# Max pooling over groups of 16: each row load split into two DMAs, issued from SyncE and ScalarE

## The chip, the cores and the metric

The kernel runs on one core of one Trainium2 chip. The metric is the device time of one execution in microseconds (us), given as the median of several runs. The profile is one further execution, recorded by the hardware profiler.

## The reference

The input `x` is 32 x 256 x 4096 in float32 (134.22 MB), and the output is 32 x 256 x 256 (8.39 MB). Each output is the maximum of 16 neighbouring inputs, because 4096 / 256 = 16:

```python
for i in range(output_size):            # 256
    start = int(i * length / output_size)
    end = int((i + 1) * length / output_size)
    result[:, :, i] = np.max(x[:, :, start:end], axis=-1)
```

## The kernel before

All the 2,097,152 windows of W = 16 elements are laid out as 128 partitions x 16,384 windows. The work is cut into 16 chunks of CHUNK = 1024 windows per partition: nine chunks form the first group, six and a last one form the second. Within a group, each partition reads one contiguous piece of memory. A full chunk is one load of 128 rows of 64 KB, 8192 KB in all.

One tile, `sb`, holds everything: a ring with two slots of CHUNK + GAP windows, and behind the ring the pooled results, which stay on the chip until the end. The order of the program is:

- A small first load (line 70) brings the final FIRST = 128 windows of each partition, 1024 KB in rows of 8 KB, into a part of the ring that the first full load does not touch, and `pooled` reduces it. What the last chunk still has to load is then 896 windows per partition, 7168 KB in rows of 56 KB. That is the "last load".
- The loop over `rows` issues 15 full loads and the last load (line 88). Load k goes to slot k % 2. Within the slot it alternates between offset 0 and offset GAP = 152 every second use (`moved`), so that load k + 2 overlaps all but 152 windows of load k, and never touches those 152.
- Each full chunk is reduced by VectorE in two instructions (line 57, inside `pooled`): first the 872 windows that load k + 2 will overwrite, then the 152 that it will not. Load k + 2 can therefore be issued as soon as the larger reduction of load k is done, while the smaller one still runs. Two loads can be outstanding at a time.
- The last load is reduced in one instruction of 896 windows.
- The output leaves in three stores: two large ones from SyncE (line 103: 4608 KB for the first group, 3072 KB for six chunks of the second) behind all loads, and one of 512 KB from ScalarE (line 100) when the last reduction is done.

All loads and the two large stores are issued by SyncE, in the order of the program. ScalarE issues only the last store and computes nothing. The tile framework puts in the waits: a load waits for the reductions that read, and the loads that wrote, what it overwrites, and a reduction waits for the loads that wrote what it reads.

Of the kernel before, what the change touches and what calls it, by code (L numbers as in the profile page):

```python
# [1 line left out]

# [4 lines left out]


@with_exitstack
def kernel(  # L10
    ctx: ExitStack,
    tc: tile.TileContext,
    x: bass.AP,
    output_size: bass.AP,
    out: bass.AP,
):
    nc = tc.nc
    P = nc.NUM_PARTITIONS
    fp32 = mybir.dt.float32

    B, C, L = x.shape
    O = int(output_size)
    assert L % O == 0, (L, O)
    W = L // O
    total = B * C * O // P
    assert B * C * O % P == 0

    xw = x.flatten_outer_dims().rearrange("r (o w) -> (r o) w", w=W)
    ow = out.flatten_outer_dims().rearrange("r o -> (r o)")
    taken = 0  # L30

    def group(n):

        nonlocal taken
        span = slice(taken * P, (taken + n) * P)
        taken += n
        return (
            xw[span].rearrange("(p n) w -> p (n w)", p=P),
            ow[span].rearrange("(p n) -> p n", p=P),
        )  # L40

    CHUNK = 1024
    GAP = 152
    FIRST = 128
    RING = 2 * (CHUNK + GAP) * W


    GROUPS = (9, 6)
    last = CHUNK - FIRST
    assert (sum(GROUPS) + 1) * CHUNK == total and last * (W + 1) <= CHUNK * W  # L50


    pool = ctx.enter_context(tc.tile_pool(name="pool", bufs=1))
    sb = pool.tile([P, RING + total - last], fp32, tag="sb", name="sb")

    def pooled(dst, at, n):
        nc.vector.reduce_max(  # L57
            out=sb[:, dst : dst + n],
            in_=sb[:, at * W : (at + n) * W].rearrange("p (n w) -> p n w", w=W),
            axis=mybir.AxisListType.X,  # L60
        )

    groups = [
        group((loads + (g == len(GROUPS) - 1)) * CHUNK) for g, loads in enumerate(GROUPS)
    ]
    assert taken == total
    x_end, o_end = groups[-1]
    cut = GROUPS[-1] * CHUNK

    nc.sync.dma_start(  # L70
        out=sb[:, CHUNK * W : (CHUNK + FIRST) * W], in_=x_end[:, (cut + last) * W :]
    )
    pooled(RING, CHUNK, FIRST)

    rows, stores = [], []
    at = RING + FIRST
    for (xg, og), loads in zip(groups, GROUPS):
        rows += [(xg, k * CHUNK, CHUNK, at + k * CHUNK) for k in range(loads)]
        if loads:
            stores.append((og[:, : loads * CHUNK], sb[:, at : at + loads * CHUNK]))  # L80
        at += loads * CHUNK
    rows.append((x_end, cut, last, None))

    for k, (xg, a, n, dst) in enumerate(rows):

        moved = k // 2 % 2
        at = k % 2 * (CHUNK + GAP) + moved * GAP
        nc.sync.dma_start(
            out=sb[:, at * W : (at + n) * W], in_=xg[:, a * W : (a + n) * W]
        )  # L90
        if dst is not None:
            mid = CHUNK - GAP if moved else GAP
            parts = [(0, mid), (mid, n)]
            for u, v in parts if moved else parts[::-1]:
                pooled(dst + u, at + u, v - u)
        else:
            assert (at + CHUNK) * W == RING
            pooled(RING - n, at, n)

    nc.scalar.dma_start(out=o_end[:, cut:], in_=sb[:, RING - last : RING + FIRST])  # L100
    tc.no_sync_barrier()
    for dst, src in stores:
        nc.sync.dma_start(out=dst, in_=src)


# [1 line left out]
_INS = ['x', 'output_size']  # L107
_OUTS = [((32, 256, 256), 'float32')]

_NUMBERS = {'output_size': 256}  # L110


# [26 lines left out]
```

## Time and profile before

| quantity | value |
|---|---|
| time, median of 3 runs | 334.65 us (334.64 to 334.85) |
| profiled execution, its own time | 334.95 us |
| span of that execution (first to last instruction) | 333.2 us |
| VectorE (DVE) busy | 276.5 us, 83% of the span |
| DMA queue q1 (SyncE's), share of 16 engines | 98.8% |
| DMA queue q10 (ScalarE's), share of 16 engines | 0.4% |
| bytes read / written | 134.22 MB / 8.39 MB |

The profiled execution spent 1.75 us outside its span, and took 0.30 us more than the median. In the profile, a "packet" is the record of one row moved by one DMA engine, or of the small completion record of 4 bytes that each of the 16 engines writes at the end of a DMA. A full load thus leaves 128 + 16 = 144 packets, eight rows and one completion record per engine. "SPq" and "ACTq" are the instruction streams of SyncE and ScalarE.

### The profile page before, as it was taken

How to read it: one execution, taken by the hardware profiler on the slowest of the kernel's cores; microseconds unless marked ns; L12 is line 12 of the kernel's file. 1: busy time of each engine (PE TensorE's matmuls, PEld its weight loads, DVE VectorE, ACT ScalarE, POOL GpSimd, SP SyncE). 2: the span in 40 equal slices, each digit the busy share in tenths (PEclk: the TensorE clock that was granted, in tenths of full speed). 3: DMA queues.
4: the chain of work that ended last, by engine and by line, in shares of the span. 5: the costliest groups of instructions: out<-in, count | busy, mean ns of one | idle time of the engine just before them, and what ended most of it. 6: DMA issues, size and time to landing. Idle time of an engine off the chain costs nothing.

```text
span 333.2 us, 113 instructions
## 1 busy us (share of the span) xinstructions
DVE 276.5 (83%) x32; POOL 0.2 (0%) x4
## 2 busy tenths in 40 slices
DVE  2009979797997979799797979979797997979994
POOL 0000000000000000000000000000000000000000
DMA  9898989899898989899898989999898989999997
GB/s 378 378 504 378 504 378 496 386 409 472 378 504 378 504 378 496 386 409 472 378 504 378 504 378 488 393 409 472 378 504 378 504 378 488 393 456 434 396 406 323
DMA packets 2880, 142.61 MB, mean 428 GB/s; under 512 B 320, under 2 KB 320, under 8 KB 448
## 3 DMA queue, kind: packets, MB, share of 16 engines
q1 hardware_dynamic: 2736, 142.08, 98.8%
q10 hardware_dynamic: 144, 0.52, 0.4%
HBM read 134.22 MB, written 8.39 MB: 428 GB/s over the span
## 4 chain that ended last, share of the span: by engine, by line
DMA 58%; DVE 36%; DVEq 5%; issue 0%; SPq 0%
DMA sb<-in_x_dram 58%; DVE sb L57 36%; DVEq L134 5%; SPq L70 0%
## 5 line engine op out<-in xcount | busy, mean ns | idle before, releaser
L57 DVE TENSOR_REDUCE sb<-sb 128x872 f32<-128x13952 f32 (+3 forms) x32 | 276.5, 8681 | 51.8 <-DMA sb<-in_x_dram 51.8
L120 POOL MEMSET const-bfloat16-1.0<- 128x1 bf16 x1 | 0.1, 102 | 0.0
L120 POOL MEMSET const-uint8-127<- 128x1 uint8 x1 | 0.1, 101 | 0.0
L120 POOL MEMSET const-float32-0.0<- 128x1 f32 x1 | 0.1, 99 | 0.2 <-issue 0.2
L120 POOL MEMSET const-float32-1.0<- 128x1 f32 x1 | 0.1, 98 | 0.0
## 6 DMA issues: line engine op xcount, KB each, us to landing
sb<-in_x_dram SPq DMA_DIRECT2D x1, 7168.0 KB, 21.6
out_dram<-sb SPq DMA_DIRECT2D x1, 4608.0 KB, 32.1
out_dram<-sb SPq DMA_DIRECT2D x1, 3072.0 KB, 17.7
sb<-in_x_dram SPq DMA_DIRECT2D x1, 1024.0 KB, 5.0
out_dram<-sb ACTq DMA_DIRECT2D x1, 512.0 KB, 4.0
sb<-in_x_dram SPq DMA_DIRECT2D x15, 24.0
```

Of the source, the lines that this page charges most:

```text
L57: nc.vector.reduce_max(out=sb[:, dst : dst + n], in_=sb[:, at * W : (at + n) * W].rearrange("p (n w) -> p n w", w=W), axis=mybir.AxisListT ...
L120: nc = _bacc.Bacc("TRN2", target_bir_lowering=False, num_devices=1)
L134: with _tile.TileContext(nc) as tc:
```

## The change

Every load of the loop goes out as two DMAs: SyncE issues the first half of the windows of each partition, ScalarE the second half. The rows of each DMA are half as long (32 KB, and 28 KB for the last load). The small first load, the reductions and the stores are as before.

```diff
         moved = k // 2 % 2
         at = k % 2 * (CHUNK + GAP) + moved * GAP
-        nc.sync.dma_start(
-            out=sb[:, at * W : (at + n) * W], in_=xg[:, a * W : (a + n) * W]
-        )
+
+        half = n // 2
+        for queue, u, v in ((nc.sync, 0, half), (nc.scalar, half, n)):
+            queue.dma_start(
+                out=sb[:, (at + u) * W : (at + v) * W], in_=xg[:, (a + u) * W : (a + v) * W]
+            )
         if dst is not None:
```

## The prediction

> **What bounds the kernel now.** I read the page first: how busy the DMA engines are, and whether anything else is near its limit.
>
> ```profile
> DVE 276.5 (83%) x32; POOL 0.2 (0%) x4
> ...
> q1 hardware_dynamic: 2736, 142.08, 98.8%
> q10 hardware_dynamic: 144, 0.52, 0.4%
> ```
>
> The 16 DMA engines are busy for almost the whole span, VectorE for 83% of it. The page's chain names 58% DMA and 36% DVE, but that is one ring slot at a time; the chain in order of time shows the period:
>
> ```profile
> 39.83 23.97 DMA sb<-in_x_dram
> 63.80 0.02 issue
> 63.82 14.70 DVE sb L57
> 78.52 0.02 issue
> 78.54 23.96 DMA sb<-in_x_dram
> ```
>
> One slot takes 38.7 us per load. With two slots, a load lands every 19.35 us. Next the windows, to see if the engines rest inside that period (columns: window, DVE busy, POOL busy, PE clock, DMA share, GB/s):
>
> ```profile
> 20.50:39.83 19.33, 14.72 (x2) 0.00 (x0) 1.00 1.00 434
> 39.83:59.18 19.35, 17.27 (x3) 0.00 (x0) 1.00 1.00 434
> ```
>
> They don't: share 1.00, 434 GB/s. Of the 23.97 us from issue to landing, 19.35 are the transfer, and the other 4.6 are mostly queueing behind the load before. That queue is the reserve. A new load's data starts moving about 1.02 us after its issue (the first issue, at 0.72, has its first packet record at 1.75), and the engines write their last row of the load before up to 1.0 us ahead of its landing (records: 43.44 on the first engine to finish, landing 44.45). So a load at 39.83 is ready at 40.85, and the engines run dry at 43.44: **a load may be issued 2.6 us later than now before an engine idles.** VectorE's own reserve is the 2.07 us it waits before each load:
>
> ```profile
> 44.47 17.28 DVE L57 TENSOR_REDUCE sb<-sb 128x872 f32<-128x13952 f32 x2 [2.08 <-DMA sb<-in_x_dram]
> 63.82 17.28 DVE L57 TENSOR_REDUCE sb<-sb 128x872 f32<-128x13952 f32 x2 [2.07 <-DMA sb<-in_x_dram]
> ```
>
> At the start there is no pooling to wait for: SyncE issues the small load and two full loads at once.
>
> ```profile
> 0.72 0.37 SPq L70 DMA_DIRECT2D sb<-in_x_dram  x1
> 1.15 0.90 SPq L88 DMA_DIRECT2D sb<-in_x_dram  x2
> 5.76 2.29 DVE L57 TENSOR_REDUCE sb<-sb 128x128 f32<-128x2048 f32 x1 [5.76 <-DMA sb<-in_x_dram]
> 25.11 14.69 DVE L57 TENSOR_REDUCE sb<-sb 128x872 f32<-128x13952 f32 x1 [17.07 <-DMA sb<-in_x_dram]
> ```
>
> In one queue, load 0 is moved completely before load 1 begins. This order is what the change gives up.
>
> **The change part by part.** *Issues.* ScalarE gains 16 DMA issues, SyncE keeps its 17 loads. An issue of a load took 0.33 to 0.43 us, and only SyncE's own issues follow it, so taking the second half to ScalarE removes nothing from the path: 0 us. ScalarE has no other work; its last store stands behind the last half load, which is issued 37 us earlier. Cover: the 2.6 us above.
>
> *Waits.* Each half load waits for the same large reduction as the whole load did. Each large reduction waits for two semaphores instead of one; the nearest row is a wait instruction of 0.02 to 0.03 us on SyncE, inside VectorE's 2.07 us of idle time: 0 us. If that cover were gone, 16 x 0.03 = 0.5 us.
>
> *Rows.* In the packet records, a 64 KB row follows the one before on its engine after 2.414 us, an 8 KB row after 0.306 us. Two points give 4.8 ns per row and 1.205 us per 32 KB. Per load an engine gets 16 rows instead of 8, and two completion records instead of one: 8 x 4.8 ns + 6 ns = 0.044 us. The engines are the bound, so 16 loads cost 16 x 0.044 = **0.7 us**. Bounds: 0, if two queues hide the step between rows, and 1.4 us, if changing queue costs as much again. I take 0.7.
>
> *The order at the start.* ScalarE leaves the opening barrier 5 ns after SyncE (0.647 against 0.642 in the instruction records), so its half of load 0 goes out together with the small load. Now each engine has two queues with work. No two queues overlap for long in this trace: q10 has only the last store, whose packets start at 330.02, when q1's last one ends. So how they share is unknown, and I bound it. If the engine takes all of a DMA before it changes, the order stays as it was: 0 us. If it takes one row from each queue in turn, the small load's eight rows of 8 KB alternate with eight of 32 KB, and all of load 0's ScalarE half is through when the small load is. ScalarE's queue is then one half load ahead. Load 0's SyncE half next alternates with *load 1's* ScalarE half:
> - small load now through at 4.80 us on the first engine; with eight 32 KB rows (8 x 1.21 = 9.67), at 14.5;
> - then 8 rounds of two 32 KB rows, 19.35 us: load 0 is through at 33.8, or 32.6 if SyncE's row goes first in each round. Before: 24.12. So it lands 8.5 to 9.7 us later, and I take 8.5, as SyncE issues first;
> - VectorE starts on it at 25.11 + 8.5 = 33.6 and is through with 872 windows at 48.3; load 2 goes out then and is ready at 49.35;
> - load 1 ends at 43.5, where it always did, since the bytes are the same. The engines idle **5.8 us** (7.0 at the other end).
>
> After that, load 2's halves start together with equal rows and stay level. VectorE ends load 1 at 50.9 + 14.7 = 65.6, load 3 is ready at 66.6, load 2 lasts until 49.35 + 19.35 = 68.7: cover 2.1 us, so no further idling. Later VectorE waits 2 us per load again, and the tail is shifted as a whole: the last reduction starts at 313.23, when VectorE is through with the chunk before, and the last load has landed 0.3 us earlier (312.95); both move by the same amount.
>
> The sum against the profiled execution: 334.95 + 0.7 + 5.8 = 341.45; less the 0.30 by which it lies over the median, **341.2 us**.
>
> The Trainium skill, "DMA: Bandwidth & Descriptors", section "Issuing engines are not separate DMA queues", speaks against the change: DMAs of several engines run on the same 16 DMA engines and interleave, and only sequencer time is saved. By that rule the gain is nil, and the trace agrees, with 98.8% busy from one queue.
>
> **The rivals.**
>
> *Whole DMAs in turn (not slower).* The engine keeps to one DMA's share (eight rows and the completion record) before it changes queue. Then the order is small load, half, half, as before, and only the rows cost: 334.65 + 0.7 = 335.35 if the step of 4.8 ns stays, 334.65 if it is hidden, 334.75 if it stays but the slow start is filled (the small load's eight rows take 3.05 us from the first packet, against 8 x 0.306 = 2.45, so at most 0.6 is to be had there). It decides from the point where a run of one queue's rows is longer than the 2.6 us of cover. For: on the last engine a q1 row still begins at 329.72, when q10's store, issued at 328.34, could have been there (329.36). Against: this is 0.36 us, less than the time of one row.
> By the Trainium skill, same page, section "Queues, rings and completion order", an engine goes round its queues packet by packet, draining typically 9 to 17 descriptors before it switches. If the nine records of a load's share on an engine are such a packet, this rival holds, with 335.35; if each row is a packet, the forecast does. No run so far shows which.
>
> *Equal bytes.* The queues share by bytes. Then the small load (64 KB per engine) puts ScalarE's queue two 32 KB rows ahead, load 0 lands 2.4 us late, which the cover of 2.6 just takes; a lead of one row may live on to the end. There the last load would land 1.2 us late, the last reduction would end at 329.5, and its store, now waiting until 330.02 for the engines, would be ready at 330.6 or later while nothing else is left to move. Price 0.7 + up to 1.4: 336.8.
>
> *Faster.* Two queues keep each engine fuller. What is to be had: the 0.6 us at the start, and 0.03 us in each of some 12 loads, which take 19.35 in the packet records instead of the first four's 19.32. At most 1.0, less what the rows cost: 334.0. Against it: the share is 1.00 already.
>
> That the change doesn't do what it says can be left out: ScalarE's instruction stream has the 16 loads.
>
> **How the numbers follow.** The measurement can tell about 0.2%, here 0.67 us: under 333.98 is faster, over 335.32 slower. Row by row: 0.50, all slower. Whole DMAs: 0.26, of which 0.13 within 0.2% (rows hidden or the start filled), 0.12 slower by a hair and 0.01 faster. Equal bytes: 0.14, slower. Fuller engines: 0.06, faster. 0.04 for something slower that I don't see, such as a lead of one queue that returns with every load. Faster 0.07, same 0.13, slower 0.80. The forecast's own range is 340.5 (start filled) to 342.6 (7.0 of idling). For 8 in 10 the range must reach down through the two cheaper ways of sharing: 334.7 to 342.4.
>
> **What would show it.** In the profile after: the small load's time to landing goes from 5.0 us to 13 or 14; the first large reduction starts at 33 to 35 instead of 25.11; the DMA row has a gap of about 6 us near 44 to 50 us, and nothing like it later; landings then come every 19.39 us; VectorE waits about 2 us before each load. If the first large reduction starts near 25, the queues don't alternate by rows, and I am wrong by 6 us. If it starts near 27.5, they share by bytes. If load 2 comes late but the gap returns with every pair of loads, the queues do not start level again, and the time is well over 343.

## The result, and the profile after

The changed kernel takes **343.97 us** (343.87 to 344.23, 4 runs), against 334.74 us for the kernel before in the same comparison: 9.23 us more, ratio 1.0275 (95% interval 1.0263 to 1.0288). The forecast was 341.2 us, with a range that ended at 342.4. The sign and the mechanism were right, the size was not. The profiled execution took 343.87 us, with a span of 341.8 us.

The page after, sections 1 and 3 (columns of the queues: packets, MB, share of 16 engines):

```profile
DVE 276.4 (81%) x32; POOL 0.2 (0%) x4
...
q1 hardware_dynamic: 2736, 75.50, 51.6%
q10 hardware_dynamic: 2448, 67.11, 45.6%
```

Together the queues now fill 97.2% of the span instead of 99.2%, and VectorE's work is the same 276 us. Most of the loss is idle DMA time. The page's row of DMA load in 40 slices shows where:

```profile
DMA  7999929999999999999999999999999999999997
```

There is one hole, in the sixth slice. The timeline of the start shows what leads up to it:

```profile
0.73 66.29 ACTq L91 DMA_DIRECT2D sb<-in_x_dram  x4
0.73 0.38 SPq L70 DMA_DIRECT2D sb<-in_x_dram  x1
...
15.24 2.29 DVE L57 TENSOR_REDUCE sb<-sb 128x128 f32<-128x2048 f32 x1 [15.24 <-DMA sb<-in_x_dram]
34.75 34.46 DVE L57 TENSOR_REDUCE sb<-sb 128x872 f32<-128x13952 f32 x4 [17.23 <-DMA sb<-in_x_dram]
71.58 14.69 DVE L57 TENSOR_REDUCE sb<-sb 128x872 f32<-128x13952 f32 x1 [2.36 <-DMA sb<-in_x_dram]
```

The small load's reduction starts at 15.24 us instead of 5.76, and load 0's at 34.75 instead of 25.11. Loads 0 and 1 are then reduced without a pause (34.46 us, four instructions): load 1 was there already. In the chain in order of time, load 2 goes out only when the first large reduction ends:

```profile
49.45 0.02 issue
49.47 22.09 DMA sb<-in_x_dram
71.56 0.02 issue
71.58 14.70 DVE sb L57
86.28 0.02 issue
86.30 24.12 DMA sb<-in_x_dram
```

Load 2 lands after 22.09 us because nothing was queued in front of it. From load 4 on a load takes 24.12 us, so the queue is full again. The windows (columns: window, DVE busy, POOL busy, PE clock, DMA share, GB/s) show the engines before and in the hole:

```profile
33.80:43.60 9.80, 8.85 (x1) 0.00 (x0) 1.00 0.99 428
43.60:50.50 6.90, 6.90 (x2) 0.00 (x0) 1.00 0.13 33
```

From the packet records, no engine has work between 43.93 and 50.42 us. On average an engine rests 6.9 us, and its first 32 KB row afterwards takes 1.66 to 2.13 us instead of 1.21. The span grew by 8.6 us, from 333.2 to 341.8, so 6.9 of it is this rest.

The records of one engine at the hand-over from the small load show how two queues are served (start in us, us, queue, bytes):

```
12.983 0.309 q1  8192    the small load's eighth row
13.289 1.213 q10 32768   the eighth row of ScalarE's half of load 0
14.499 0.009 q1  4       the small load's completion record
14.505 0.009 q10 4       the half load's completion record
14.510 1.213 q1  32768   first row of SyncE's half of load 0
15.720 1.213 q10 32768   first row of ScalarE's half of load 1
```

The queues take turns row by row, an 8 KB row against a 32 KB row. A completion record is a turn of its own: the small load's data is through at 13.29, but its record waits for the other queue's row and is written at 14.50.

### The profile page after: what moved, and what is told of

It is laid out like the page before. It is cut to its first block, busy times and chain, and to the rows that moved or that the text cites. A ratio compares the mean times of both kernels' runs of the same rounds, so it can differ in the third digit from the quotient of the medians.

```text
span 341.8 us, 157 instructions
## 1 busy us (share of the span) xinstructions
DVE 276.4 (81%) x32; POOL 0.2 (0%) x4
## 4 chain that ended last, share of the span: by engine, by line
DMA 59%; DVE 35%; DVEq 4%; issue 0%; SPq 0%
DMA sb<-in_x_dram 59%; DVE sb L57 35%; DVEq L137 4%; SPq L70 0%; DVEq L57 0%
## 6 DMA issues: line engine op xcount, KB each, us to landing
sb<-in_x_dram ACTq DMA_DIRECT2D x15, 4096.0 KB, 24.1
sb<-in_x_dram SPq DMA_DIRECT2D x1, 1024.0 KB, 14.5
```

## The experiments

**Start level.** The small load is split too, so that neither queue gets ahead.

```diff
-    nc.sync.dma_start(
-        out=sb[:, CHUNK * W : (CHUNK + FIRST) * W], in_=x_end[:, (cut + last) * W :]
-    )
+    for queue, u, v in ((nc.sync, 0, FIRST // 2), (nc.scalar, FIRST // 2, FIRST)):
+        queue.dma_start(
+            out=sb[:, (CHUNK + u) * W : (CHUNK + v) * W],
+            in_=x_end[:, (cut + last + u) * W : (cut + last + v) * W],
+        )
```

> The changed kernel, but the small first load is split in two halves like the others (SyncE and ScalarE, eight rows of 4 KB per engine each), so that both queues start level. Theory (the queues take one row in turn, and the small load on SyncE's queue alone lets ScalarE's queue run one half load ahead, which idles the engines once, near 44 to 50 us): load 0 lands near 25 again, no gap, only the dearer rows are left: 335.4 to 336.1 us. Rival (two queues fall out of step by themselves, or cost in every load): the time stays above 340 us.

Measured: 336.41 us against 334.73, ratio 1.0048 (1.0035 to 1.0060). Its timeline:

```profile
25.14 17.28 DVE L57 TENSOR_REDUCE sb<-sb 128x872 f32<-128x13952 f32 x2 [17.31 <-DMA sb<-in_x_dram]
44.59 17.28 DVE L57 TENSOR_REDUCE sb<-sb 128x872 f32<-128x13952 f32 x2 [2.17 <-DMA sb<-in_x_dram]
```

Load 0 is back at 25.14, load 1 at 44.59, and there is no hole. All 16 loads still go out as halves from two engines, so 7.6 of the 9.2 us hang on the order at the start. The rest, 1.68 us, is 0.3 us over the upper end of what was expected.

**Whole loads first.** Loads 0 and 1 whole from SyncE, halves from load 2 on.

```diff
-        for queue, u, v in ((nc.sync, 0, half), (nc.scalar, half, n)):
+        halves = ((nc.sync, 0, half), (nc.scalar, half, n))
+        for queue, u, v in halves if k >= 2 else ((nc.sync, 0, n),):
```

> The changed kernel, but loads 0 and 1 go out whole from SyncE; the halves on two queues begin with load 2. Theory (all of the big loss is the order at the start): first large reduction at 25.1 us, no gap, 335.3 to 336.0 us. Rival (the halves cost in every load): with 14 of 16 loads still in halves, most of the 9.2 us stays, above 341 us.

Measured: 336.26 us against 334.73, ratio 1.0049 (1.0035 to 1.0063). The first large reduction starts at 24.69:

```profile
24.69 17.28 DVE L57 TENSOR_REDUCE sb<-sb 128x872 f32<-128x13952 f32 x2 [17.05 <-DMA sb<-in_x_dram]
```

The total is 0.3 us over the upper end of the expected. 14 loads in halves cost only 1.5 us, so the 9.2 us are not a price paid in every load.

**Halves first.** The opposite: only loads 0 and 1 as halves.

```diff
+        halves = ((nc.sync, 0, half), (nc.scalar, half, n))
+        for queue, u, v in halves if k < 2 else ((nc.sync, 0, n),):
```

> The kernel before, but loads 0 and 1 alone go out as halves from SyncE and ScalarE. Theory: the whole gap is back with only two of 16 loads changed: load 0 lands near 34.8, engines idle 6.6 us and take 0.9 us to come back to speed, 334.7 + 7.5 + 0.1 = 342.3 us. Rival (cost spread over all loads): 2/16 of 9.2 us, 335.9 us.

Measured: 342.63 us against 334.73, ratio 1.0235 (1.0221 to 1.0249): 7.90 us.

```profile
34.78 34.47 DVE L57 TENSOR_REDUCE sb<-sb 128x872 f32<-128x13952 f32 x4 [17.22 <-DMA sb<-in_x_dram]
71.43 14.69 DVE L57 TENSOR_REDUCE sb<-sb 128x872 f32<-128x13952 f32 x1 [2.19 <-DMA sb<-in_x_dram]
```

The changed kernel's start is here to within 0.2 us, with two loads of 16 changed.

**One queue.** Both halves from SyncE, one behind the other.

```diff
-        for queue, u, v in ((nc.sync, 0, half), (nc.scalar, half, n)):
+        for queue, u, v in ((nc.sync, 0, half), (nc.sync, half, n)):
```

> The changed kernel, but both halves of every load go out from SyncE, one behind the other: the same rows and DMAs in one queue, so that nothing is taken in turn. Theory: no gap; the price of 32 KB rows alone, 16 x 0.044 = 0.7 us, 335.4 us; if the further 0.04 us per load that the changed kernel's period shows (19.43 instead of 19.39 us) belongs to the rows and not to changing queue, 335.9 us. Rival (halving the loads is what costs, whatever the queue): above 341 us.

Measured: 335.83 us against 334.73, ratio 1.0029 (1.0018 to 1.0041): 1.10 us for twice the rows and DMAs alone. Two pieces of its chain, two loads apart:

```profile
59.54 23.74 DMA sb<-in_x_dram
...
98.39 23.75 DMA sb<-in_x_dram
```

98.39 - 59.54 = 38.85 us for two loads, 19.43 each, the same as in the changed kernel. The price above the 0.7 us of the forecast belongs to the short rows, not to changing queues. The packet records agree: with one queue a half load takes 9.68 us at first and 9.71 from about 55 us on, and in the changed kernel more than half of the 32 KB rows follow each other after 1.213 to 1.219 us instead of 1.209 from about 90 us on.

The kernel before slows too. On its first engine the completion records of the loads come 19.32 us apart up to 82 us, and 19.35 afterwards. Spread over the eight rows of a load that is about 4 ns per row, and the halves have sixteen: 19.36 us at first, 19.42 to 19.43 later. So the halves cost 0.043 us per load at first, which is what the forecast had, and 0.077 later. From the small load's completion record to that of the last load, the engine that is ahead takes 307.1 us in the kernel before and 308.3 with one queue, 1.2 us more where 0.7 was forecast. Why rows become slower in the course of a run is not known.

**The dose.** If rows are served in turn, load 0 is late by eight of ScalarE's rows, so the loss must follow their length. SyncE takes three quarters, or one quarter, of each load:

```diff
-        half = n // 2
+        half = n * 3 // 4        # the other kernel: n // 4
```

> The changed kernel, split at three quarters: SyncE's rows are 48 KB, ScalarE's 16 KB. Theory (one row in turn, whatever its length): until the small load's eight rows are through, ScalarE's queue moves eight rows of 16 KB, so load 0 is late by half of what it was, 8 x 0.61 = 4.8 us, lands near 29.9, and the engines idle 2.2 us and restart slowly (0.9): 334.7 + 1.1 for the rows + 3.1 + up to 0.4 = 338.9 to 339.3 us. Rival (what counts is that two queues start unequal, or bytes are shared equally): the start does not get cheaper by the shorter rows, 343 to 344 us by the first, 336 to 337 by the second.

> The other way: SyncE's rows are 16 KB, ScalarE's 48 KB. Theory: load 0 is late by 8 x 1.8 = 14.5 us, the engines idle 11.8 us and restart in 0.9: 334.7 + 1.1 + 12.7 + up to 0.4 = 348.5 to 348.9 us. Rivals as for three quarters: 343 to 344, or 336 to 337 us.

Measured, against 334.81: 347.27 us (344.69 to 349.72), ratio 1.0345 (1.0288 to 1.0402), for three quarters; 361.81 us, ratio 1.0789 (1.0768 to 1.0810), for one quarter. Both miss, the first even in the order: a smaller imbalance was slower than the even split. The timeline of the three quarters says why:

```profile
66.96 17.28 DVE L57 TENSOR_REDUCE sb<-sb 128x152 f32<-128x2432 f32 x2 [2.54 <-DMA sb<-in_x_dram]
86.36 17.28 DVE L57 TENSOR_REDUCE sb<-sb 128x152 f32<-128x2432 f32 x2 [2.13 <-DMA sb<-in_x_dram]
108.71 17.28 DVE L57 TENSOR_REDUCE sb<-sb 128x872 f32<-128x13952 f32 x2 [5.07 <-DMA sb<-in_x_dram]
```

Two of the merged lines begin with the 152 windows instead of the 872. In the even split the small reduction also needs only one of the two DMAs, and the large one both, but there the large one comes first in all 15 full loads. With unequal parts the framework's scheduler put the small one first in 7 of the 15. The load that waits for the large reduction then goes out 2.6 us later, which is the whole of the 2.6 us of cover. Load 4's reduction at 108.71 has waited 5.07 us. The four runs lie in two pairs, near 344.8 and 349.7 us, and the trace is of the slower pair; what sets them apart is not shown. In the one-quarter kernel it is worse, since VectorE takes the small reduction of load 1 before the large one of load 0:

```profile
39.63 2.69 DVE L57 TENSOR_REDUCE sb<-sb 128x152 f32<-128x2432 f32 x1 [17.14 <-DMA sb<-in_x_dram]
44.52 31.87 DVE L57 TENSOR_REDUCE sb<-sb 128x152 f32<-128x2432 f32 x3 [2.20 <-DMA sb<-in_x_dram]
```

So both were run again with the order of the reductions held:

```diff
             for u, v in parts if moved else parts[::-1]:
                 pooled(dst + u, at + u, v - u)
+                tc.no_sync_barrier()
```

> The split at three quarters again, with the order of VectorE's reductions held to that of the changed kernel (the larger one first in every load; in the run without this it came second in half of the loads, so that the load after it went out 2.6 us later). Theory (a row in turn, and the swapped order took the cover): load 0 lands near 29.9, one gap of 2.2 us plus 0.9, then none: 338.9 to 339.3 us. Rival (queues with unequal rows get out of level by themselves later on): 344 to 350 us, as without the order held.

> The split at one quarter with the same order of reductions held. Theory: load 0 lands 14.5 us late near 39.6, one gap of 11.8 us plus 0.9: 348.5 to 348.9 us. Rival: 360 us or more, as without the order held.

Measured: 338.88 us against 335.09, ratio 1.0115 (1.0098 to 1.0132), and 348.68 us, ratio 1.0407 (1.0392 to 1.0423). The first is at the lower end of what was expected (338.9), the second inside it. But the kernel before took 335.09 us here and not the 334.7 of the expectations: the losses, 3.79 and 13.59 us, are 0.4 and 0.2 us under the least that was expected. First three quarters, then one quarter:

```profile
29.86 34.47 DVE L57 TENSOR_REDUCE sb<-sb 128x872 f32<-128x13952 f32 x4 [17.23 <-DMA sb<-in_x_dram]
66.67 17.28 DVE L57 TENSOR_REDUCE sb<-sb 128x872 f32<-128x13952 f32 x2 [2.35 <-DMA sb<-in_x_dram]
```

```profile
39.65 34.46 DVE L57 TENSOR_REDUCE sb<-sb 128x872 f32<-128x13952 f32 x4 [17.22 <-DMA sb<-in_x_dram]
76.50 17.28 DVE L57 TENSOR_REDUCE sb<-sb 128x872 f32<-128x13952 f32 x2 [2.38 <-DMA sb<-in_x_dram]
```

With the changed kernel between them, the table has three doses. "Late" is the start of the first large reduction less 25.11 us, "loss" the time over the kernel before in the same comparison, and "start's share" the loss less the 1.10 us of the short rows:

| ScalarE's rows | late | loss | start's share | late less share |
|---|---|---|---|---|
| 16 KB | 4.75 | 3.79 | 2.69 | 2.1 |
| 32 KB | 9.64 | 9.23 | 8.13 | 1.5 |
| 48 KB | 14.54 | 13.59 | 12.49 | 2.1 |

From the first dose to the last, 9.8 us of lateness cost 9.8 us. What is forgiven is about 2 us: the cover of 2.6 less a slow restart of about 0.7. The packet records show the cover by itself: an engine rests 2.1, 6.9 and 11.8 us on average, in each dose 2.7 to 2.8 us less than load 0 is late. The even split loses 0.5 us more than the other two doses give. That does not lie in its rest, and it was timed in another comparison, without the lines that hold the order (a run of the even split with them was not made).

**The small load from ScalarE**, all else as in the kernel before:

```diff
-    nc.sync.dma_start(
+    nc.scalar.dma_start(
         out=sb[:, CHUNK * W : (CHUNK + FIRST) * W], in_=x_end[:, (cut + last) * W :]
```

> The kernel before, all loads whole from SyncE; only the small load goes out from ScalarE, at the same time as load 0. Theory (a row in turn): the small load's rows now stand between 64 KB rows and it lands near 22 us instead of 5.7, which still leaves VectorE time before load 0 at 25.1; no gap, no dearer rows: 334.7 us, or up to 0.6 us less if two queues fill the slow start. Rival (two unequal queues at the start cost by themselves): several us more.

Measured: 337.88 us (337.11 to 338.47) against 334.81, ratio 1.0087 (1.0073 to 1.0100). The expectation missed:

```profile
25.40 36.66 DVE L57 TENSOR_REDUCE sb<-sb 128x128 f32<-128x2048 f32 x5 [25.40 <-DMA sb<-in_x_dram]
66.71 14.69 DVE L57 TENSOR_REDUCE sb<-sb 128x872 f32<-128x13952 f32 x1 [4.65 <-DMA sb<-in_x_dram]
```

SyncE's row goes first on every engine, so the small load's eighth row stands behind load 0's eighth: it begins at 23.8 us on the first engine, and the completion record comes at 24.1, not near 22. VectorE must do the small reduction first, so load 0's starts 2.6 us late (25.40 + 2.29, against 25.11), about the whole cover. That puts the next load's first row at the moment the engines run dry: issued at 42.31, with 1.02 us to the first row, against 43.42. By the packet records seven engines go on without a pause and nine rest 0.4 to 2.7 us, whose first 64 KB row then takes 2.75 to 3.26 us instead of 2.41. Load 2 ends 1.1 us later than before on the first engine and 3.0 us later on the last. Running just dry was not free; why the nine engines got their first row only 2.1 to 3.9 us after the issue is not shown. The slow start wasn't filled either: on the first engine the rows of the small load and of load 0 were all through at 24.09 us, against 24.11.

**Whole loads in turn**, even ones from SyncE and odd ones from ScalarE:

```diff
-        nc.sync.dma_start(
+        (nc.scalar if k % 2 else nc.sync).dma_start(
             out=sb[:, at * W : (at + n) * W], in_=xg[:, a * W : (a + n) * W]
```

> The kernel before with whole loads of 64 KB rows, but even loads go out from SyncE and odd ones from ScalarE. Theory (a row in turn): loads 0 and 1 share the engines and land together near 44 us, both slots are then reduced with little in flight, and this returns with every pair: about 379 us, engines idle 17 us near 43 to 60 us and 2 us in every pair after that. Rival (an engine finishes a DMA before it changes queue): 334.7 us.

Measured: 356.6 us (355.5 and 357.71) against 334.81, ratio 1.0649 (1.0619 to 1.0680).

```profile
25.03 16.88 DVE L57 TENSOR_REDUCE sb<-sb 128x128 f32<-128x2048 f32 x2 [25.03 <-DMA sb<-in_x_dram]
44.37 19.87 DVE L57 TENSOR_REDUCE sb<-sb 128x872 f32<-128x13952 f32 x3 [2.46 <-DMA sb<-in_x_dram]
```

The rival is out: in the packet records the small load's 8 KB rows stand one by one between the 64 KB rows of ScalarE's load 1. The size missed by 22 us, for two reasons. Load 1 took its eight turns beside the small load and was through at 24.1, a whole load early. And the scheduler gave VectorE another order again, load 1's large reduction ahead of load 0's, which put the early load to use; the expectation had kept the old order.

## Why the prediction was wrong, point by point

- *Queueing bounds the kernel, with 2.6 us of cover.* Right: the rests of the three doses give 2.7 to 2.8 us of cover, and 2.6 us late was just too late in the run with the small load on ScalarE.
- *Issues and waits cost nothing.* No run shows a price inside the span for ScalarE's issues or the second wait: VectorE's idle time before a load stays at 2.07 to 2.4 us, and the kernel that starts level has the same span as the one with a single queue, 334.2 us in both profiles.
- *A row from each queue in turn; load 0 late; one hole; level afterwards.* Right: the small load landed after 14.5 us (13 or 14 forecast), the first large reduction started at 34.75 (33 to 35), the hole lay at 43.9 to 50.4 us, and no other followed. Of the signs that were named, only the period was off, 19.43 us instead of 19.39; that belongs to the rows below.
- *The size of the hole.* This is the step that failed first. Of the two ends, 8.5 and 9.7 us, I took 8.5 "as SyncE issues first". SyncE's row did go first. But a load counts as landed when its completion record is written, and that record stood behind one more ScalarE row of 1.21 us. Load 0 was 9.64 us late, the other end of the bounds, and the engines idled 6.9 us instead of 5.8.
- *The restart.* It had no term, the second step that failed. The prediction knew that a cold start is slow (0.6 us for the small load), booked it as a possible gain, and did not book the second cold start that its own hole makes: 0.45 to 0.92 us on the first row of each engine.
- *The rows.* 0.7 us forecast; the single-queue kernel measured 1.10, within the bounds of 0 to 1.4. The 4.8 ns per row came from rows early in the run. The prediction knew that later loads take 0.03 us more, but booked it as a gain for fuller engines, not as a price that doubles when each load has twice the rows.
- *The sum.* 1.1 for the hole, about 0.7 for the restart and 0.4 for the rows bring the forecast's 6.5 us to 8.7. By whole kernels, the start alone (7.90) and the rows alone (1.10) give 9.0 of the 9.23 us, with the short rows of loads 0 and 1, about 0.1 us, in both. The remainder stays open: about 0.3 us here, 0.6 us between the level start (336.41) and the single queue (335.83). Most of it lies outside the span, where the profiled executions of the changed kernel and of the level start spend 2.07 and 2.2 us, against 1.75 us before and 1.8 us with halves first and with the single queue.
- *The range* ended at the unfavourable end of one term (334.65 + 0.7 + 7.0 = 342.35), with nothing for a restart on top; that is why it missed by 1.6 us. Two figures beside it do not follow from their terms: 342.6 for 7.0 us of idling, and 334.0 for the rival of fuller engines, whose gain of 1.0 less 0.7 for the rows gives 334.35, not faster by the prediction's own limit.
- *The rivals.* Whole DMAs in turn is refuted by the packet records and by the loads in turn; equal bytes by the records and the three doses; fuller engines by the runs at 336.3 and 336.4 us and by the slow start, which stayed. The Trainium skill, "DMA: Bandwidth & Descriptors", section "Queues, rings and completion order", holds here if a row is its packet; its figure of typically 9 to 17 descriptors per turn does not, since a turn in these packet records was one row of 8 to 64 KB or one completion record. The Trainium skill, same page, section "Issuing engines are not separate DMA queues", is borne out: no kernel with loads on two queues was faster than the one before (336.26 us at best, against 334.73).

## What to carry to other kernels

Splitting each load over two issuing engines added no bandwidth here, where one queue already kept the DMA engines 98.8% busy; what it changed was the order in which loads finished. If the queues take a row each in turn, a queue with short rows in front holds its next transfer back by as many rows of the other queue as it has, so start both queues level, or keep what must land first in one queue with what comes after. When a forecast contains an idle gap, book the restart behind it, count the completion record as a turn of its own, and look whether a change of tile boundaries has made the scheduler reorder the consumers.

## What the runs showed that I had not expected

- A completion record of 4 bytes waits its turn behind a row of the other queue: 1.21 us with 32 KB rows in the changed kernel, and one 64 KB row (2.41 us) with whole loads in turn.
- After 6.9 us without work, an engine's first 32 KB row took 1.66 to 2.13 us instead of 1.21.
- Moving one edge of a split reordered VectorE's reductions and cost 8.4 us (347.27 against 338.88, with the four unordered runs from 344.69 to 349.72) and 13.1 us (361.81 against 348.68).
- When load 2 arrived just as the engines ran dry, nine of the 16 rested up to 2.7 us, and the run lost 3.1 us (337.88 against 334.81).
